# All score products over 128 rows, and the residual held in two tiles

## The chip, the core and the metric

The kernel runs on one core of a Trainium2 chip. The metric is the device time of one execution in microseconds (us).

## The reference

One decoder layer runs for a prompt of 1024 tokens and for 8 sequences of 4 new tokens each (1056 columns together). Differential attention and an RG-LRU recurrence share one input projection and one output projection; a gated ConvFFN follows. The prompt's attention, cut to what matters here:

```python
def diff_attn_block(q, k, v, mask, lam):
    s = jnp.einsum('bqhcd,bkhcd->bhcqk', q.astype(F32), k.astype(F32)) * (QK_SUB_DIM ** -0.5)
    s = jnp.where(mask, s, jnp.finfo(F32).min)
    p = jax.nn.softmax(s, axis=-1)
    p_diff = p[:, :, 0] - lam * p[:, :, 1]
    return jnp.einsum('bhqk,bkhd->bqhd', p_diff, v.astype(F32))
...
    m = jnp.concatenate([attn_out, lru_out], axis=-1) @ p['w_out']
    x = x + gt1 * m
```

There are 4 heads, each with 2 sub-heads `c` of 64 features. `x` is the residual; `gt1` comes from the modulation vector.

## The kernel before

A float32 matrix product is made of three products (`mm3`, lines 154 to 157): each operand is split into a high and a low part of type fp32r, and high x high, high x low and low x high are summed in PSUM. The stages follow one another: `front` normalises x, projects, runs the recurrence beside the projections, projects the values (`v_block`) and runs the prompt's attention; `output` runs the output projection with the sample attention beside it, and then the feed-forward part, which takes half of the time.

**The attention** runs over 16 groups `g`, four for each head; `pr = g % 4` is a pair of 128-query blocks. Each group has four score tiles `score(g, x, c)` with x and c in 0, 1, and each score tile is built of `pr + 1` pieces of up to 256 keys. A piece has two products. The first (line 744) contracts over 128 rows: the tile `QA` holds the 64 high features of a query and, in the other 64 rows, its low part, and `KA` holds the key's high part twice. The second (line 745) is high query x low key, and contracts over the 64 rows `me` of the sub-head alone. A bf16 product (line 746) adds the causal mask. That makes 160 products of each of the first two kinds.

A score tile lies in one of two PSUM buffers (`s_ps`). VectorE reduces its maximum (line 750), ScalarE takes the exponential (line 752), and with that the buffer is free. `combine` subtracts the two sub-heads on VectorE; `pv_T` transposes the result in TensorE, ScalarE and VectorE split it; `pv` multiplies with the values `vh`, `vl` into one PSUM buffer `pv_ps`, which ScalarE copies to `oT` and sends to DRAM (lines 795 to 797). Between the score tiles TensorE also does the projections of queries and keys three groups ahead (`qk_mm`, `qk_norm`) and the transposes of the next group (`qk_T`). `qk_norm` ends on GpSimd with the rotary part, which uses a scratch tile `rp` (lines 662 to 676); for pr = 2 the same is done for the 32 sample rows (`qk_ss`).

**The residual** is one tile `x2` of 128 x 8 x 1056. It stands where the values and the attention's tiles lie before, so `output` can load it only when the attention has ended (`x2_load`, line 1153). `accumulate` (line 1084) adds a product of the output projection to it. The first such group of products, `wo_first`, runs in the PSUM buffers of the score tiles during the end of the attention; the sample attention (`sa_pn`, `sa_ps`) takes these PSUM buffers after it.

What sets the order: the program is written in order, and a scheduler with a timeline model of its own then moves instructions on every engine, the DMA queue included. On the chip each engine runs its instructions strictly in the order that results.

Of the kernel before, what the change touches and what calls it, by code (L numbers as in the profile page):

```python
# [144 lines left out]
class Build:  # L145
# [56 lines left out]
    def front(self):  # L202
# [159 lines left out]
        lamb = self.load(lp, "lru_lambda", [128, 4])  # L362
        wgh = ada.tile([128, 2, 4, 128], F32R, name="wgh")
        wgl = ada.tile([128, 2, 4, 128], F32R, name="wgl")
        lco = lp.tile([128, 4, 27], F32, name="lco")
# [116 lines left out]
        e = lp.tile([128, 4, 4], F32, name="sp_e")  # L482
# [62 lines left out]
        evac(3, b)  # L545
        W.split_to(7)
# [41 lines left out]
        vpp = pool("v", side="right")  # L588
# [41 lines left out]
        SP.dma_start(a["lru_conv_o"], lco)  # L630
# [47 lines left out]
        PS, ST, QA, KA, KL = {}, {}, {}, {}, {}  # L678
        qbank = [lambda: bank("qk_ps", "mm", 6)]
# [15 lines left out]
        def qk_T(g):  # L695
# [9 lines left out]
            for c in range(2):  # L705
                S.activation(qa[me[c], c], b[me[c], 0], AF.Copy, scale=0.125)
            for c in range(2):
                S.activation(ka[me[c], c], b[me[c], 1], AF.Copy)
                S.activation(ka[me[1 - c], c], b[me[c], 1], AF.Copy)
# [24 lines left out]
        def score(g, x, c):  # L734
# [3 lines left out]
            me = slice(64 * c, 64 * c + 64)  # L738
            q = QA[g][:, c, x * 128:(x + 1) * 128]
            for kp in range(pr + 1):  # L740
# [4 lines left out]
                PE.matmul(o, q[me], KL[4 * h + kp][me, :w], start=False, stop=not last, skip_group_check=True)  # L745
# [5 lines left out]
            e = EX[g, x, c] = p.tile([128, 1024], F32, name="p_e", tag=f"p_e{c}", bufs=4 if c == 0 else 2)  # L751
# [29 lines left out]
        def pv(g, b):  # L781
# [12 lines left out]
            if last:  # L794
                ot = p.tile([128, 256], F32, name="oT", tag="oT", bufs=1)
# [21 lines left out]
        for g in range(NG):  # L817
# [82 lines left out]
        vpp.__exit__(None, None, None)  # L900
        self.psb = psp
# [170 lines left out]
    def output(self):  # L1072
        a, V, S, G, PE, SP, W = self.a, self.V, self.S, self.G, self.PE, self.SP, self.W
        pool, act_at = self.pool, self.act_at
        xpp = pool("x2", side="right")
        x2 = xpp.__enter__().tile([128, NK, T], F32, name="x2")
# [3 lines left out]
        def accumulate(b, m, i, gt, pl):  # L1080
# [3 lines left out]
            V.scalar_tensor_tensor(x2[:, m, t0:t0 + w], b[:, :w], gt[:, m, 0:1], x2[:, m, t0:t0 + w], op0=ALU.mult, op1=ALU.add)  # L1084
            if tw > w:
# [3 lines left out]
                V.tensor_tensor(x2[:, m, SEQ:], t, x2[:, m, SEQ:], op=ALU.add)  # L1089

        def norm2(i, env, acc):
# [15 lines left out]
            if tw > w:  # L1107
                ts = p.tile([128, NK, SAMP], F32, name="u2s", tag=tags[0], bufs=2)
                V.tensor_tensor(ts, x2[:, :, SEQ:], bc[:, None, w:tw].to_broadcast([128, NK, SAMP]), op=ALU.mult)
# [463 lines left out]
```

## Time and profile before

| | us |
|---|---|
| median of 3 runs | 1433.25 (1430.48 to 1434.02) |
| the profiled execution | 1431.46 |
| its span, first to last instruction | 1429.6 |
| TensorE busy | 1380.3 (97%) |
| VectorE, ScalarE, GpSimd busy | 810.8, 553.5, 427.3 |

The profile's engines are PE (TensorE matmul), PEld (its weight loads), DVE (VectorE), ACT (ScalarE), POOL (GpSimd) and SP (the queue that issues most DMAs). The recorded end of a matmul is modelled and overlaps the next one, so what a matmul costs is read from the distance of two starts, not from its duration. Stages in the span: up to 245 us projections and recurrence, 245 to 498 us the score tiles, then the end of the attention and the output projection up to 690 us, then the feed-forward part.

### The profile page before, as it was taken

The numbers are of one execution on the slowest core, as the hardware profiler recorded it, in microseconds if no ns is written. First come the engines' busy times: TensorE is split into PE (matmuls) and PEld (weight loads), VectorE is DVE, ScalarE is ACT, GpSimd is POOL, SyncE is SP. The second block draws the span as 40 slices with busy tenths as digits, with TensorE's granted clock in tenths as the row PEclk, the third lists the DMA queues.
The fourth block names the chain that finished last, engine by engine and source line by source line (L and its number), as shares of the span: only waits on it lengthen the run. The fifth ranks groups of instructions, "written<-read, shape, count | busy, mean of one in ns | idle before, by whom it ended". The sixth has DMA issues, their size and how long they took to land.

```text
span 1429.6 us, 23840 instructions
## 1 busy us (share of the span) xinstructions
PE 1380.3 (97%) x9520; PEld 1302.9 (91%) x9520; DVE 810.8 (57%) x1700; ACT 553.5 (39%) x981; POOL 427.3 (30%) x504
## 2 busy tenths in 40 slices
PE   3998999999999989999999999999999999999998
PEld 3898999788878777789999999999999999999998
DVE  5759534876667436578764545353545353635356
ACT  4366623554545532326723232314141414142411
POOL 1162114433334022413633232314141414142320
PEclk8999999998999899999999999999999999999999
DMA  8625351101011287502111010102020202020203
GB/s 337 253 91 182 144 186 56 50 16 45 20 42 58 70 299 245 187 29 72 45 45 60 30 60 31 60 30 60 30 70 20 75 16 75 15 74 17 73 16 133
DMA packets 51936, 121.99 MB, mean 85 GB/s; under 512 B 8274, under 2 KB 25554, under 8 KB 48754
## 3 DMA queue, kind: packets, MB, share of 16 engines
q1 hardware_dynamic: 46914, 115.73, 24.1%
q10 hardware_dynamic: 4912, 4.74, 1.0%
q8 instruction: 75, 1.23, 0.4%
q14 instruction: 35, 0.29, 0.1%
HBM read 106.51 MB, written 13.94 MB: 84 GB/s over the span
## 4 chain that ended last, share of the span: by engine, by line
PE 89%; DVE 6%; ACT 2%; DMA 2%; issue 1%; POOL 0%; SPq 0%; DVEq 0%; ACTq 0%; POOLq 0%
PE up L155 12%; PE up L156 12%; PE up L157 12%; PE dn L157 6%; PE dn L156 6%; PE dn L155 6%; PE s_ps L745 3%; PE qk_ps L155 3%; PE qk_ps L156 3%; PE qk_ps L157 3%; PE s_ps L744 2%; PE wo_ps L155 2%; PE wo_ps L157 2%; PE wo_ps L156 1%; PE qk_pt L774 1%
## 5 line engine op out<-in xcount | busy, mean ns | idle before, releaser
L60 POOL TENSOR_TENSOR w_lo<-w_raw,w_hi 128x1024 fp32r<-128x1024 f32 x90 | 223.7, 2494 | 592.4 <-ACT w_hi L59 500.9
L155 PE MATMUL up<-act_h,w_hi 128*128 128x384 f32 (+1 forms) x1056 | 341.4, 324 | 1.9 <-ACT act_h L1129 1.9
L157 PE MATMUL up<-act_h,w_lo 128*128 128x384 f32 (+1 forms) x1056 | 340.2, 323 | 0.8 <-DVE w_lo L60 0.8
L156 PE MATMUL up<-act_l,w_hi 128*128 128x384 f32 (+1 forms) x1056 | 340.8, 323 | 0.0
L1084 DVE SCALAR_TENSOR_TENSOR x<-dn,modT,x 128x384 f32<-128x384 f32 (+1 forms) x264 | 149.6, 570 | 167.9 <-PE dn L157 167.7
L1306 DVE SCALAR_TENSOR_TENSOR fy<-fx,conv_ffn_w,fy 128x1072 f32<-128x1072 f32 (+2 forms) x92 | 137.9, 1500 | 173.2 <-ACT fy L1304 171.9
L155 PEld LDWEIGHTS up<-act_h,w_hi 128*128 128x128 f32 x1056 | 197.9, 188 | 2.4 <-ACT act_h L1129 2.2
L157 PEld LDWEIGHTS up<-act_h,w_lo 128*128 128x128 f32 x1056 | 198.3, 188 | 1.1 <-DVE w_lo L60 1.1
L59 ACT ACTIVATE w_hi<-w_raw 128x1024 fp32r<-128x1024 f32 x94 | 98.0, 1057 | 261.7 <-PE dn L156 151.3
L156 PEld LDWEIGHTS up<-act_l,w_hi 128*128 128x128 f32 x1056 | 198.3, 188 | 0.0
L157 PE MATMUL dn<-hh,w_lo 128*128 128x384 f32 (+1 forms) x528 | 170.5, 323 | 0.0
L156 PE MATMUL dn<-hl,w_hi 128*128 128x384 f32 (+1 forms) x528 | 170.5, 323 | 0.0
L155 PE MATMUL dn<-hh,w_hi 128*128 128x384 f32 (+1 forms) x528 | 169.7, 321 | 0.0
L155 PEld LDWEIGHTS dn<-hh,w_hi 128*128 128x128 f32 x528 | 99.2, 188 | 0.0
L157 PEld LDWEIGHTS dn<-hh,w_lo 128*128 128x128 f32 x528 | 99.1, 188 | 0.0
L156 PEld LDWEIGHTS dn<-hl,w_hi 128*128 128x128 f32 x528 | 99.1, 188 | 0.0
L155 PE MATMUL qk_ps<-w_hi,act_h 128*128 128x256 f32 (+1 forms) x288 | 85.9, 298 | 0.0
L157 PE MATMUL qk_ps<-w_hi,act_l 128*128 128x256 f32 (+1 forms) x288 | 84.1, 292 | 0.0
L156 PE MATMUL qk_ps<-w_lo,act_h 128*128 128x256 f32 (+1 forms) x288 | 84.1, 292 | 0.0
L750 DVE TENSOR_REDUCE ls<-s_ps 128x1 f32<-128x128 f32 (+7 forms) x64 | 48.1, 755 | 54.1 <-PE s_ps L746 53.8
L155 PE MATMUL wo_ps<-act_h,w_hi 128*128 128x384 f32 (+1 forms) x192 | 62.7, 338 | 2.8 <-ACT p_e L752 1.1
L156 PE MATMUL wo_ps<-act_l,w_hi 128*128 128x384 f32 (+1 forms) x192 | 62.4, 326 | 0.0
(323 smaller groups left out, 2653.4 us busy)
## 6 DMA issues: line engine op xcount, KB each, us to landing
w_ada<-w_ada SPq DMA_DIRECT2D x24, 1024.0 KB, 6.3
w_raw<-w_up SPq DMA_DIRECT2D x44, 512.0 KB, 3.6
w_raw<-w_down SPq DMA_DIRECT2D x22, 512.0 KB, 3.5
w_raw<-w_in SPq DMA_DIRECT2D x20, 512.0 KB, 3.7
page<-cache_v SPq DMA_DIRECT2D x32, 256.0 KB, 5.0
xT<-xT SPq DMA_DIRECT2D x8, 528.0 KB, 7.9
w_raw<-w_out SPq DMA_DIRECT2D x8, 512.0 KB, 3.8
kp<-cache_k SPq DMA_DIRECT2D x16, 256.0 KB, 4.7
```

The costliest lines, as they stand in the source:

```text
L59: self.nc.scalar.activation(hi, self.raw[i], AF.Copy)
L60: (eng or self.nc.gpsimd).tensor_tensor(lo, self.raw[i], hi.bitcast(F32), op=ALU.subtract)
L155: self.PE.matmul(out, lh, rh, start=first, stop=False)
L156: self.PE.matmul(out, lh, rl, start=False, stop=False)
L157: self.PE.matmul(out, ll, rh, start=False, stop=last)
L744: PE.matmul(o, q, KA[4 * h + kp][:, c, :w], start=True, stop=False, skip_group_check=True)
L745: PE.matmul(o, q[me], KL[4 * h + kp][me, :w], start=False, stop=not last, skip_group_check=True)
L750: V.tensor_reduce(l[:, c:c + 1], b[:, :n], axis=AX.X, op=ALU.max, negate=True)
L774: PE.transpose(t[:, o:o + 128], PD[g, x][:, (2 * b + kk) * 128:(2 * b + kk + 1) * 128], ident)
L1084: V.scalar_tensor_tensor(x2[:, m, t0:t0 + w], b[:, :w], gt[:, m, 0:1], x2[:, m, t0:t0 + w], op0=ALU.mult, op1=ALU.add)
L1306: post.append(lambda c0=c0, c1=c1, j=j: V.scalar_tensor_tensor(y[:, c0:c1], x[:, c0 + j:c1 + j], fw[:, ci, j:j + 1], y[:, c0:c1], op0=ALU. ...
```

## The change

The low-key product gets a query tile `QZ` in which the 64 rows of the other sub-head are zero, so that it too contracts over 128 rows; two such tiles exist, zeroed once, and GpSimd copies the high query part into them in each group. The residual becomes two tiles of 128 x 4 x 1056. The first, `x2a`, takes the place of the values of heads 0 and 1, which are dead by group 9, and is loaded whole there; the second, `x2b`, is loaded in `output` in two pieces. To make room, the exponentials get tiles of their true width (still four and two of them), `oT` shares the one scratch tile of the rotary part (tag `rp`), and a few small tiles of the recurrence move to another pool, with their loads and arithmetic earlier. The line numbers of the changed kernel are larger by 4 to 18.

```diff
-        vh = [vp.tile([128, 8, 256], F32R, name=f"vh{b}") for b in range(2)]
-        vl = [vp.tile([128, 8, 256], F32R, name=f"vl{b}") for b in range(2)]
+        v01 = x2p.tile([128, 4 * T], F32R, name="v0", tag="v", bufs=1)[:, :4096]
+        v01 = [v01.rearrange("p (z t c) -> p z t c", z=2, t=8), vp.tile([128, 2, 8, 256], F32R, name="v1")]
+        vh, vl = ([t[:, z] for t in v01] for z in range(2))
...
+        QZ = [p.tile([128, 2, 256], F32R, name=f"QZ{i}") for i in range(2)]
+        for t in QZ:
+            G.memset(t.bitcast(F32), 0.0)
...
             for c in range(2):
+                G.tensor_copy(QZ[g % 2][me[c], c], qa[me[c], c])
...
-                PE.matmul(o, q[me], KL[4 * h + kp][me, :w], start=False, stop=not last, skip_group_check=True)
+                PE.matmul(o, qz, KL[4 * h + kp][:, :w], start=False, stop=not last, skip_group_check=True)
...
-            e = EX[g, x, c] = p.tile([128, 1024], F32, name="p_e", tag=f"p_e{c}", bufs=4 if c == 0 else 2)
+            e = EX[g, x, c] = p.tile([128, ((6, 8)[pr % 2 or c] - 1 + x) * 128], F32, name="p_e",
+                                     tag=f"p_e{c}{x}{'' if c else pr % 2}", bufs=1)
...
-                ot = p.tile([128, 256], F32, name="oT", tag="oT", bufs=1)
+                ot = p.tile([128, 256], F32, name="oT", tag="rp", bufs=1)
...
+            if g == 9:
+                self.x2 = [x2p.tile([128, 4, T], F32, name="x2a", tag="v", bufs=1)]
+                SP.dma_start(self.x2[0], a["xT"][0:4].rearrange("m p t -> p m t"))
...
-        x2_load(0, 4, 0, 384)
+        x2_load(0, 384)
...
-            x2_load(4, 4, 0, 384)
-            x2_load(0, 4, 384, T - 384)
-            x2_load(4, 4, 384, T - 384)
+            x2_load(384, T - 384)
```

Three places in the order of the built programs. On TensorE, at the end of the attention, before the change (`wo_ps` are the output projection's first group, `sa_pn` and `sa_ps` the sample attention):

```order
L155 MATMUL wo_ps<-act_h_66,w_hi 128x384
L156 MATMUL wo_ps<-act_l_67,w_hi 128x384
L157 MATMUL wo_ps<-act_h_66,w_lo 128x384
L992 MATMUL sa_pn<-ksT,qblk 32x32 x4
L998 MATMUL sa_ps<-kp,qblk 32x128
L992 MATMUL sa_pn<-ksT,qblk 32x32 x12
```

The same place with the change; the last two rows stand 31 rows behind the others, with products of the projection's second group between:

```order
L157 MATMUL wo_ps<-act_h_66,w_lo 128x384
L1201 MATMUL o_ms<-ident,le 12x128
L155 MATMUL wo_ps<-act_h_66,w_hi 128x384
L156 MATMUL wo_ps<-act_l_67,w_hi 128x384
...
L155 MATMUL wo_ps<-act_h_66,w_hi 128x384
L1007 MATMUL sa_pn<-ksT,qblk 32x32 x16
```

The sample attention's first products have moved behind products of the next projection group, which use other PSUM buffers.

On ScalarE, at the turn from group 6 to group 7, before the change (`oT` is the output of group 5, `qk_st` the projection for group 9):

```order
L752 ACTIVATE p_e_4004,ls_3946<-s_ps_3995,ls_3946 128x768
L796 ACTIVATE oT_4048<-pv_ps_3988 128x256
L797 DMA scr_o<-oT_4048 128x256
L649 ACTIVATE qk_st_4063<-qk_ps_3916 128x512
L651 ACTIVATE qk_sq_4065<-qk_ps_3916 128x512
L752 ACTIVATE p_e_4142,ls_4140<-s_ps_4130,ls_4140 128x896
```

And with the change:

```order
L762 ACTIVATE p_e_4025,ls_3965<-s_ps_4016,ls_3965 128x768
L653 ACTIVATE qk_st_4084<-qk_ps_3935 128x512
L655 ACTIVATE qk_sq_4086<-qk_ps_3935 128x512
L762 ACTIVATE p_e_4163,ls_4161<-s_ps_4151,ls_4161 128x896
L806 ACTIVATE oT_4069<-pv_ps_4009 128x256
L807 DMA scr_o<-oT_4069 128x256
```

The copy to `oT` now stands behind three more instructions, and in front of the exponential of group 7's second score tile.

On GpSimd, around the sample rows' rotary part in group 6 with the change (`QZ_2238` is the zero-padded query tile of group 7; before the change the three COPY rows are not there, and the rest stands in the same order):

```order
L716 COPY QZ_2237<-QA 64x256 x2
L60 TENSOR_TENSOR w_lo<-w_raw,w_hi 128x1024 x2
L716 COPY QZ_2238<-QA 64x256
L666 TENSOR_TENSOR qk_st<-qk_st,qk_ms 128x512
L716 COPY QZ_2238<-QA 64x256
L670 TENSOR_TENSOR qk_st<-qk_st,g_qk 128x256 x2
L666 TENSOR_TENSOR qk_ss<-qk_ss,qk_ms 32x256
```

The second copy for group 7 stands behind a normalisation that waits for VectorE.

## Rows read from the trace of the kernel before

**Rows 1.** The page: span, busy time by engine, and the chain that ended last.

```profile
span 1429.6 us, 23840 instructions
PE 1380.3 (97%) x9520; PEld 1302.9 (91%) x9520; DVE 810.8 (57%) x1700; ACT 553.5 (39%) x981; POOL 427.3 (30%) x504
PE 89%; DVE 6%; ACT 2%; DMA 2%; issue 1%; POOL 0%; SPq 0%; DVEq 0%; ACTq 0%; POOLq 0%
```

**Rows 2.** Windows: the score tiles, head 0's alone, the boundary; columns in the first line.

```profile
core 0: us, PE busy (x) PEld busy (x) DVE busy (x) ACT busy (x) POOL busy (x), PEclk, DMA share, GB/s
245.00:497.90 252.90, 250.39 (x1536) 208.16 (x1537) 176.56 (x512) 137.56 (x322) 85.22 (x130) 0.93 0.13 40
245.00:300.00 55.00, 54.06 (x345) 43.83 (x346) 44.07 (x125) 30.56 (x76) 21.11 (x31) 1.00 0.11 32
497.90:520.60 22.70, 17.58 (x117) 16.74 (x117) 8.70 (x15) 8.73 (x16) 6.29 (x10) 0.99 0.76 251
```

**Rows 3.** Timeline of TensorE, 441 to 446 us: start, duration, instruction.

```profile
441.03 0.28 PE L157 MATMUL qk_ps<-w_hi,act_l 128*128 128x256 f32 x1
...
442.45 0.28 PE L157 MATMUL qk_ps<-w_hi,act_l 128*128 128x256 f32 x1
...
443.96 0.28 PE L157 MATMUL qk_ps<-w_hi,act_l 128*128 128x256 f32 x1
444.08 0.28 PE L744 MATMUL s_ps<-KA,QA 128*128 128x256 f32 x1
444.29 0.38 PE L745 MATMUL s_ps<-KL,QA 64*128 64x256 f32 x1
444.60 0.49 PE L744 MATMUL s_ps<-KA,QA 128*128 128x128 f32 x2
445.02 0.38 PE L745 MATMUL s_ps<-KL,QA 64*128 64x256 f32 x1
445.33 0.33 PE L744 MATMUL s_ps<-KA,QA 128*128 128x128 f32 x1
```

**Rows 4.** Lines 744 and 745: count, duration (min, median, max), forms.

```profile
L744 PE MATMUL s_ps<-KA,QA x160: 219/364/581, 245.0 to 497.0; 128*128 128x256 f32 x128, 128*128 128x128 f32 x32
L745 PE MATMUL s_ps<-KL,QA x160: 322/381/579, 245.2 to 497.3; 64*128 64x256 f32 x128, 64*128 64x128 f32 x32
```

**Rows 5.** Windows of single groups: group 2 (head 0), group 7, group 15.

```profile
264.80:280.30 15.50, 15.17 (x96) 12.11 (x94) 15.23 (x41) 7.89 (x20) 9.05 (x9) 1.00 0.29 85
345.60:366.10 20.50, 20.50 (x105) 16.43 (x104) 12.65 (x33) 8.46 (x17) 7.30 (x15) 0.83 0.05 14
478.00:497.90 19.90, 19.90 (x84) 14.89 (x83) 7.67 (x13) 9.11 (x14) 0.00 (x0) 0.74 0.22 71
```

**Rows 6.** Waits in 245 to 500 us: total us, times, longest.

```profile
DVE ls L750 <- PE s_ps L746: 53.8, 40, 4.5
POOL qk_st L662 <- DVE qk_ms L142: 26.9, 6, 12.4
```

**Rows 7.** GpSimd groups, 245 to 500 us: busy us, mean ns, idle before.

```profile
L662 POOL TENSOR_TENSOR qk_st<-qk_st,qk_ms 128x512 f32<-128x512 f32 x14 | 14.6, 1045 | 90.2 <-DVE qk_ms L142 26.9 <-issue 21.3 <-ACT ksT L863 15.1
L675 POOL TENSOR_TENSOR rp<-qk_st,rope 128x64 f32<-128x64 f32 x14 | 4.5, 319 | 0.0
```

**Rows 8.** Timelines of ScalarE and GpSimd at 344 to 352 and 411 to 418 us.

```profile
344.27 0.38 ACT L796 ACTIVATE oT<-pv_ps 128x256 f32<-128x256 f32 x1 [3.56 <-PE pv_ps L157]
351.02 0.31 POOL L676 TENSOR_TENSOR qk_ss<-rp 32x64 f32<-32x64 f32 x1
411.65 0.38 ACT L796 ACTIVATE oT<-pv_ps 128x256 f32<-128x256 f32 x1 [3.57 <-PE pv_ps L157]
417.75 0.31 POOL L676 TENSOR_TENSOR qk_ss<-rp 32x64 f32<-32x64 f32 x1
```

**Rows 9.** Timeline of the boundary, 514 to 521 us.

```profile
514.26 0.39 SPq L1154 DMA_DIRECT2D x<-xT  x1
514.69 0.51 SPq L1150 DMA_DIRECT2D gsubT<-g_sub_col  x1
519.36 2.19 DVE L1084 SCALAR_TENSOR_TENSOR x<-wo_ps,modT,x 128x384 f32<-128x384 f32 x4 [7.10 <-DMA gsubT<-g_sub_col]
520.65 0.34 PE L992 MATMUL sa_pn<-ksT,qblk 128*32 128x32 f32 x8 [4.12 <-DVE x L1084]
```

More of the change, by code (lines that the diff above doesn't have):

```diff
@@ L361, in front @@
         lcs = self.load(lp, "state_lru_conv", [128, 4, NS, 3])
-        lamb = self.load(lp, "lru_lambda", [128, 4])
+        lamb = self.load(ada, "lru_lambda", [128, 4])
         wgh = ada.tile([128, 2, 4, 128], F32R, name="wgh")
         wgl = ada.tile([128, 2, 4, 128], F32R, name="wgl")
-        lco = lp.tile([128, 4, 27], F32, name="lco")
+        lco = ada.tile([128, 4, 27], F32, name="lco")
         lho = lp.tile([128, 4, 9], F32, name="lho")
@@ L481, in front @@
         sp = lp.tile([128, 2, 4], F32, name="sp")
-        e = lp.tile([128, 4, 4], F32, name="sp_e")
+        e = ada.tile([128, 4, 4], F32, name="sp_e")
         hb = lp.tile([128, 2, 4], F32, name="hb")
@@ L545, in front @@
         evac(3, b)
+        SP.dma_start(a["lru_conv_o"], lco)
         W.split_to(7)
@@ L587, in front @@
         self.pages = []
-        vpp = pool("v", side="right")
+        self.x2p = pool("v", side="right")
+        x2p = self.x2p.__enter__()
+        vpp = pool("stage", side="right")
         vp = vpp.__enter__()
-        vh = [vp.tile([128, 8, 256], F32R, name=f"vh{b}") for b in range(2)]
-        vl = [vp.tile([128, 8, 256], F32R, name=f"vl{b}") for b in range(2)]
+        v01 = x2p.tile([128, 4 * T], F32R, name="v0", tag="v", bufs=1)[:, :4096]
+        v01 = [v01.rearrange("p (z t c) -> p z t c", z=2, t=8), vp.tile([128, 2, 8, 256], F32R, name="v1")]
+        vh, vl = ([t[:, z] for t in v01] for z in range(2))
         def stage(name):
@@ L629, in front @@
         lpp.__exit__(None, None, None)
-        SP.dma_start(a["lru_conv_o"], lco)
         SP.dma_start(a["lru_h_o"], lho)
@@ L706, in qk_T @@
                 S.activation(qa[me[c], c], b[me[c], 0], AF.Copy, scale=0.125)
+            for c in range(2):
+                G.tensor_copy(QZ[g % 2][me[c], c], qa[me[c], c])
             for c in range(2):
@@ L737, in score @@
             b = sbank("s_ps")
-            me = slice(64 * c, 64 * c + 64)
-            q = QA[g][:, c, x * 128:(x + 1) * 128]
+            q, qz = (t[:, c, x * 128:(x + 1) * 128] for t in (QA[g], QZ[g % 2]))
             for kp in range(pr + 1):
@@ L900, in front @@
         vpp.__exit__(None, None, None)
+        self.x2bp = pool("x2b", side="right")
+        self.x2.append(self.x2bp.__enter__().tile([128, 4, T], F32, name="x2b"))
         self.psb = psp
@@ L1074, in output, with x2 @@
         pool, act_at = self.pool, self.act_at
-        xpp = pool("x2", side="right")
-        x2 = xpp.__enter__().tile([128, NK, T], F32, name="x2")
+        def x2(m, c0, c1):
+            return self.x2[m > 3][:, m - 4 * (m > 3), c0:c1]
         steps = Steps()
@@ L1108, in norm2 @@
                 ts = p.tile([128, NK, SAMP], F32, name="u2s", tag=tags[0], bufs=2)
-                V.tensor_tensor(ts, x2[:, :, SEQ:], bc[:, None, w:tw].to_broadcast([128, NK, SAMP]), op=ALU.mult)
+                for z, (m0, m1) in enumerate(((0, 4), (4, NK))):
+                    V.tensor_tensor(ts[:, m0:m1], self.x2[z][:, :, SEQ:],
+                                    bc[:, None, w:tw].to_broadcast([128, m1 - m0, SAMP]), op=ALU.mult)
             ut = None
@@ L1151, in output, with x2_load @@
         V.tensor_scalar(gsubT, gsubT, 1.0 - LAM0, None, op0=ALU.mult)
-        def x2_load(m, n, t0, tw):
-            SP.dma_start(x2[:, m:m + n, t0:t0 + tw], a["xT"][m:m + n, :, t0:t0 + tw].rearrange("m p t -> p m t"))
-        x2_load(0, 4, 0, 384)
+        def x2_load(t0, tw):
+            SP.dma_start(self.x2[1][:, :, t0:t0 + tw], a["xT"][4:, :, t0:t0 + tw].rearrange("m p t -> p m t"))
+        x2_load(0, 384)
         for m in range(4):
@@ L1238, in output @@
             self.lru_cat_stage(1, stage)
-            V.tensor_copy(x2[:1, 4:, 0:1], gsubT[:1, None].to_broadcast([1, 4, 1]))
-            V.tensor_copy(x2[:1, :, 384:385], gsubT[:1, None].to_broadcast([1, NK, 1]))
-            x2_load(4, 4, 0, 384)
-            x2_load(0, 4, 384, T - 384)
-            x2_load(4, 4, 384, T - 384)
+            for t0 in (384,):
+                V.tensor_copy(self.x2[1][:1, :, t0:t0 + 1], gsubT[:1, None].to_broadcast([1, 4, 1]))
+            x2_load(384, T - 384)
             for i in range(3):
@@ L1439, in output @@
             SP.dma_start(a["ffn_conv_o"], fo)
-        xpp.__exit__(None, None, None)
+        self.x2bp.__exit__(None, None, None)
+        self.x2p.__exit__(None, None, None)
         self.sqp.__exit__(None, None, None)
```

12 lines of the change are left out of this document (6 added, 6 removed).

## The prediction

> **What bounds the kernel now.** I read the page first: TensorE is busy 97% of the span, and the chain that ended last runs through it for 89% [rows 1]. So the question in each stage is what TensorE's own instructions cost, and where it stands still. Next the windows by stage: from 245 to 497.9 us, the score tiles, TensorE is busy 250.4 of 252.9 us, while VectorE has 176.6, ScalarE 137.6 and GpSimd 85.2 [rows 2]. TensorE is the bound there, but "busy" hides how well it is used; for that I took the timeline, start against start. From 441.03 to 442.45 us thirteen products of 256 columns over 128 rows follow each other: 12 steps in 1.42 us, 0.118 us each [rows 3]. A score product of the same width does not go at that pace: the first one starts at 444.08 as usual, the 64-row one follows after 0.21, and what follows that comes after 0.31; further on the 64-row product again takes 0.31 (445.02 to 445.33) [rows 3]. So what is slow is the passage from 128 rows to 64 and back, paid by both neighbours. The recorded durations say the same: no 64-row product is under 322 ns, and the 128-row one on the same tiles goes down to 219 [rows 4]. There are 160 of each [rows 4]. The last view is the boundary of attention and output projection: TensorE idles 4.12 us before the sample attention's first product, for a VectorE accumulation that itself waited 7.10 us for a small DMA behind the residual's load [rows 9].
>
> **The score products.** A pair met alone in other 128-row work takes 0.21 + 0.31 = 0.52 us and would take 0.24, so 0.28 is saved; inside a run of pairs both starts are 0.31 apart, 0.62 against 0.24, so 0.38. Times 160 that is 45 and 61 us. Runs and single pairs are mixed, and 32 pairs have only 128 columns; I take the middle, 0.33 a pair, **-53 us**. The new product has as many columns as before and adds no instruction on TensorE. One statement of the Trainium skill speaks against this term: "TensorE: Matmul & The Clock Gate" says in the section "Part 2: What happens when you issue a matmul" that the number of rows does not matter for a weight load, and in the table of "Why this matters for your kernels" that a product over 32 rows alone takes as long as one over 128; by that the term would be zero. The Trainium skill's "TensorEngine Tiling (Array Packing)", section "Key Properties", says on the other side that a change of the tiling mode drains the engine. The 0.31 against 0.118 above is on the side of the second, and no row here shows a 64-row product between 64-row ones, which would part the two.
>
> **What the other engines take of it.** With 53 us less, TensorE would need 200 us for this stage, and VectorE's 176.6 us are then 88% of it. Today VectorE waits 53.8 us in all for the last product of a score tile [rows 6]; that slack is what goes. The bounds: no loss, because in group 2 VectorE is busy 15.23 of 15.50 us and TensorE still 15.17 [rows 5]; and at the other end the share that VectorE reaches in head 0, its best whole head, 44.07 of 55 us or 80% [rows 2]: 176.6 / 0.80 = 221 us, a loss of 21. I take **+8**, nearer to the first, because VectorE's queue was laid out by a model and group 2 shows that it can run full.
>
> **The copies into QZ.** 32 copies of 64 x 256 on GpSimd. No such row exists; a two-operand instruction on 128 x 64 takes 319 ns and one on 128 x 512 takes 1045 [rows 7], so 10 to 33 us on an engine with 85 of 253 us busy. They hide beside TensorE's work for the group before. What is late if they don't: the copy for the second sub-head in pr = 3 stands behind a normalisation that waits for VectorE (26.9 us of such waits in all [rows 6]), and the score tiles of c = 1 and all behind them on TensorE wait for it. Zero to three places at up to 1.05 us each: **+1**.
>
> **oT on the rotary scratch tile.** The copy out of `pv_ps` now waits on ScalarE until GpSimd has finished with `rp`, and the exponentials, the next group's QA and KA stand behind it; TensorE waits for those when both score buffers are full. In group 6 the copy ran at 344.27 and the sample rows' rotary part ended at 351.33, 7.1 us later; in group 10, 411.65 and 418.06, 6.4 us [rows 8]. In the other heads the two meet or don't collide. The built order already puts the copy behind `qk_st`, `qk_sq` and an exponential, some 2 us. From 0 to 13.5 us; I take **+4**.
>
> **The clock.** The granted clock is 0.93 of 2.4 GHz over the stage [rows 2], and 0.83 and 0.74 in groups 7 and 15 [rows 5], the ones with most 64-row products; with levels of 1.2 and 2.4 GHz, 0.07 x 2 x 252.9 = 35 us ran at the lower one. At most half of that, 17 us, is lost, and the score products' part of it is in the term above already, so 0 to 10 us are left. If it fell for their pace, the change gives it back. Since it may fall again where TensorE waits for VectorE, I take **-3**.
>
> **The boundary.** The accumulations of `wo_first` go into `x2a`, which has been in place since group 9, so they no longer wait for the 0.79 MB of the first piece; and the sample attention's first products stand behind products of the next projection group, which use other PSUM buffers. The 4.12 us go: **-4** (0 to -5). `gsubT` still arrives late, but only VectorE's next instructions wait for it. The 2.2 MB load of `x2a` runs while DMA is 13% busy [rows 2], in the SP queue behind stores that wait for GpSimd today as well; nothing but the accumulations at the boundary needs it. The smaller p_e tiles rotate as before, and the recurrence's few early instructions replace the same ones later: both zero. The feed-forward part is built in the same order: zero.
>
> **The sum.** -53 + 8 + 1 + 4 - 3 - 4 = -47 us. The profiled execution took 1431.46 us (span 1429.6), which gives 1384.5; the median of the runs is 1.8 us above the profiled one, so 1386. A difference under 0.3%, 4 us, is about what a measurement of this kernel can't tell from none.
>
> **The rivals.**
>
> *VectorE and ScalarE become the bound.* The two in-order queues hand each other the two score buffers, and TensorE waits for the exponential of the tile before the last. For it: VectorE at 88%, and 13 us of ScalarE waits at the upper bound. Against it: group 2. At the upper ends, 21 + 3 + 13.5 in place of 8 + 1 + 4, the gain is 47 - 24.5 = 22 and the time 1411; 1402 to 1416 is its field.
>
> *The whole price comes back, and the clock with it.* No loss to other engines, 61 us for the products, 8 for the clock, 5 at the boundary: -74 us, 1359. Against it is VectorE: its 176.6 us leave no more than 76 for the stage. Field 1358 to 1370.
>
> *The row count isn't what costs.* If what TensorE pays lies in the score tile itself (its PSUM buffer, its accumulation), the products stay at 0.31, and the boundary alone is gained: 1429. For it: both neighbours of a 64-row product are in the same buffer as it. Against it: the projection's three products also accumulate in one buffer, at 0.118 [rows 3], and the 128-row score product started 0.12 after the product ahead. By the Trainium skill's "TensorE: Matmul & The Clock Gate" ("Why this matters for your kernels") this would be the outcome: no gain on 160 pairs.
>
> *Slower than before.* The shared `rp` tile, on ScalarE: if each `oT` waits for a rotary part as in groups 6 and 10, ScalarE stands 6.4 to 7.1 us, 6.75 in the mean, with the exponentials behind it. Up to 7 such stops take back the 47 us; with all 16, 108 us, less the 4 in the sum, the time is 1386 + 104 = 1490. Against it: in the groups with pr = 1 the rotary part ahead of the copy belongs to an earlier group, and the scheduler moved copies back; it decides from 8 full stops on.
>
> **How the numbers follow.** My forecast, 1370 to 1402, gets 0.66; the VectorE and ScalarE rival 0.18; the full price 0.08; the row count 0.04; slower 0.04. The range of 8 in 10 takes the forecast, most of the second and some of the third: 1368 to 1414. Faster by over 0.3% are the first three, 0.92; the row count lies at 4 us, half to each side but by its mechanism within 0.3%: 0.04; slower 0.04.
>
> **What would show it.** In the changed profile: starts of score products 0.12 us apart; the score stage at about 210 us with VectorE over 80% busy; granted clock above 0.93; ScalarE idle before `oT` put down to GpSimd under 10 us in all; no idle time before `sa_pn`. The prediction is wrong if the products stay 0.31 apart, if TensorE waits over 25 us in this stage for exponentials or for QZ, or if the output projection, whose order changed, loses more than the boundary gives.

## The result and the profile after

The changed kernel takes 1400.0 us (median of four runs, 1397.67 to 1400.61), the kernel before 1431.9 on the same chip: 0.9775 of it, 95% interval 0.9754 to 0.9796. That is 32 us gained where the sum said 47; 1400 lies in the range, at the slow end of the forecast's own field. The profiled execution has a span of 1398.2 us, 31.4 less than before [rows 1].

The page of the changed kernel, the rows that answer to [rows 1]: span, busy time by engine, and the chain that ended last.

```profile
span 1398.2 us, 23889 instructions
PE 1324.9 (95%) x9520; PEld 1279.5 (92%) x9520; DVE 831.2 (59%) x1700; ACT 552.3 (39%) x981; POOL 449.4 (32%) x538
PE 77%; DVE 13%; ACT 4%; DMA 3%; issue 2%; POOL 0%; SPq 0%; ACTq 0%; DVEq 0%; POOLq 0%
```

VectorE's share of the chain went from 6 to 13%, and VectorE and GpSimd are busy for 20 and 22 us more than before, though VectorE has as many instructions as before (1700) and GpSimd only 34 more (the 32 copies and two memsets). The windows of the changed kernel, with the columns of [rows 2], say where: the score tiles, the boundary, and the output projection up to the first product into `up`, with which the feed-forward part begins.

```profile
245.00:470.50 225.50, 197.85 (x1540) 188.11 (x1541) 191.55 (x510) 136.21 (x321) 102.63 (x161) 0.95 0.19 58
470.50:497.00 26.50, 23.76 (x150) 22.46 (x148) 13.55 (x25) 9.26 (x20) 4.86 (x10) 1.00 0.62 201
497.00:622.50 125.50, 124.61 (x1055) 102.81 (x1055) 80.34 (x250) 39.52 (x89) 40.72 (x36) 1.00 0.45 155
```

The first row against [rows 2]: the score stage is 27.4 us shorter (225.5 for 252.9). TensorE is busy for 52.5 us less (197.9 for 250.4), but stands still for 27.6 us where it stood for 2.5, so 25.1 us of the gain are lost again. VectorE's busy time didn't stay at 176.6; it is 191.6. Boundary and output projection together take 152.0 us; before, the first product into `up` started at 654.0, 156.1 us behind the end of the score stage. So 4.1 us came from there, and the feed-forward part is as long as before (775.7 and 775.6 us). The balance is -52.5 + 25.1 - 4.1 = -31.5 us.

The products themselves do what was forecast. TensorE's timeline in the last score tile, where such products had steps of 0.21 and 0.31 before [rows 3]:

```profile
469.38 0.28 PE L753 MATMUL s_ps<-KA,QA 128*128 128x256 f32 x1
469.50 0.28 PE L754 MATMUL s_ps<-KL,QZ 128*128 128x256 f32 x1
469.62 0.28 PE L753 MATMUL s_ps<-KA,QA 128*128 128x256 f32 x1
469.74 0.28 PE L754 MATMUL s_ps<-KL,QZ 128*128 128x256 f32 x1
469.86 0.28 PE L753 MATMUL s_ps<-KA,QA 128*128 128x256 f32 x1
```

Every start is 0.12 us behind the one ahead. Who ends TensorE's idle time in the stage stands in the view of waits of the changed kernel (total us, times, longest):

```profile
PE s_ps L753 <- DVE QA L721: 10.9, 5, 2.6
PE s_ps L753 <- ACT p_e L762: 4.5, 6, 1.8
PE qk_pt L784 <- DVE KL L724: 3.8, 3, 1.7
PE qk_ps L155 <- ACT gl L819: 3.1, 1, 3.1
PE pv_ps L155 <- ACT pTh L787: 2.2, 3, 1.7
```

Before, the longest entry was

```profile
PE s_ps L744 <- DVE QA L711: 1.6, 1, 1.6
```

and VectorE's wait for the end of a score tile, 53.8 us in [rows 6], is almost gone in the changed kernel:

```profile
DVE ls L759 <- PE s_ps L755: 7.9, 8, 2.7
```

Some 17 of TensorE's 27.6 us end with VectorE, most of the rest with ScalarE. What fills VectorE is the question of the experiments.

### The profile page after: what moved, and what is told of

It reads as the page before. It is cut to its first block, busy times and chain, and to the rows that moved or that the text cites. A ratio compares the mean times of both kernels' runs of the same rounds, so it can differ in the third digit from the quotient of the medians.

```text
span 1398.2 us, 23889 instructions
## 1 busy us (share of the span) xinstructions
PE 1324.9 (95%) x9520; PEld 1279.5 (92%) x9520; DVE 831.2 (59%) x1700; ACT 552.3 (39%) x981; POOL 449.4 (32%) x538
## 3 DMA queue, kind: packets, MB, share of 16 engines
q1 hardware_dynamic: 46386, 115.73, 24.5%
## 4 chain that ended last, share of the span: by engine, by line
PE 77%; DVE 13%; ACT 4%; DMA 3%; issue 2%; POOL 0%; SPq 0%; ACTq 0%; DVEq 0%; POOLq 0%
PE up L155 12%; PE up L156 12%; PE up L157 12%; PE dn L157 6%; PE dn L156 6%; PE dn L155 6%; PE wo_ps L155 1%; PE qk_ps L155 1%; PE qk_ps L156 1%; PE qk_ps L157 1%; PE wo_ps L156 1%; PE wo_ps L157 1%; DVE ls L759 1%; PE ada_ps L266 1%; PE v_ps L155 1%
## 5 line engine op out<-in xcount | busy, mean ns | idle before, releaser
L155 PEld LDWEIGHTS up<-act_h,w_hi 128*128 128x128 f32 x1056 | 197.9, 188 | 2.5 <-ACT act_h L1147 2.3
L1100 DVE SCALAR_TENSOR_TENSOR x2a<-dn,modT,x2a 128x384 f32<-128x384 f32 (+1 forms) x132 | 74.3, 567 | 98.5 <-PE dn L157 98.5
L1100 DVE SCALAR_TENSOR_TENSOR x2b<-dn,modT,x2b 128x384 f32<-128x384 f32 (+1 forms) x132 | 75.4, 573 | 69.4 <-PE dn L157 69.2
L155 PE MATMUL qk_ps<-w_hi,act_h 128*128 128x256 f32 (+1 forms) x288 | 85.8, 298 | 0.2 <-ACT qk_sq L655 0.2
L762 ACT ACTIVATE p_e<-s_ps,ls 128x128 f32<-128x128 f32 (+7 forms) x64 | 47.5, 743 | 47.1 <-DVE ls L759 42.3
```

Source lines behind the costliest of these rows:

```text
L155: self.PE.matmul(out, lh, rh, start=first, stop=False)
L762: S.activation(e[:, :n], b[:, :n], AF.Exp, bias=l[:, c:c + 1], accum_out=l[:, 2 + c:3 + c])
L1100: V.scalar_tensor_tensor(x2(m, t0, t0 + w), b[:, :w], gt[:, m, 0:1], x2(m, t0, t0 + w), op0=ALU.mult, op1=ALU.add)
```

## The experiments

Each edit is made in the program, and the scheduler then builds the order of the instructions anew, so an experiment can change the order on several engines besides what its edit says. One figure in the expectations needs a word: the *stretch* of VectorE. For every VectorE instruction of the score stage I took its duration, less that of the shortest tenth among those with the same tiles, operation and shape, and added up what was over 0.05 us; each excess is put down to the GpSimd line that ran beside it longest. It is 16.5 us before (8.9 beside the weight splits `w_lo`) and 35.2 in the changed kernel (16.5 beside `w_lo`, 16.2 beside the norms' multiplications and the rotary part, 2.5 beside the QZ copies).

**1. The residual's part alone.** QZ and its copies are left out of the changed kernel, and its products are those of before; the smaller `p_e` tiles and the shared `oT` tile stay. The product's line:

```diff
-                PE.matmul(o, qz, KL[4 * h + kp][:, :w], start=False, stop=not last, skip_group_check=True)
+                PE.matmul(o, q[me], KL[4 * h + kp][me, :w], start=False, stop=not last, skip_group_check=True)
```

> The changed kernel with the score products over 64 rows as before: no QZ and no copies into it, the rest of the change (residual in two tiles, oT on the rotary scratch tile, smaller p_e tiles) stays. If the two parts add up, this one gives only what the boundary and the output projection gave, 156.3 us before and 152.2 after from the last score product to the first up product: 4.1 us, so 1428, and a score stage of 252 to 253 us with TensorE at 250. Rival: the 2.2 MB load of x2a or the other order costs something in the score stage that the faster products hid or made up for: 1432 or more.

Measured 1439.6 us, 1.0058 (1.0038 to 1.0079) of before: 0.6% slower, clear of the noise. The window of its score stage:

```profile
246.20:507.70 261.50, 253.84 (x1529) 207.82 (x1529) 185.73 (x511) 138.24 (x324) 90.57 (x131) 0.92 0.20 63
```

The parts don't simply add up. Boundary and output projection give 2 us (154.1 from the last score product to the first `up`), but the score stage is 8.6 us longer: TensorE is idle for 7.7 us, where it was 2.5, and busy for 3.4 more at a lower clock (0.92). VectorE is busy for 9 us more, and its stretch is 26.0 us. Half of the loss, 4.6 us, was there when the ninth group began (at 371.9), ahead of the load of `x2a`, issued at 396.2.

**2. The products' part alone.** The kernel before with QZ, its copies, the 128-row products, the `p_e` tiles and `oT` as in the change:

```diff
-                PE.matmul(o, q[me], KL[4 * h + kp][me, :w], start=False, stop=not last, skip_group_check=True)
+                PE.matmul(o, qz, KL[4 * h + kp][:, :w], start=False, stop=not last, skip_group_check=True)
```

> The kernel before with the 128-row score products, the QZ copies, the smaller p_e tiles and oT on the rotary scratch tile, and the residual as before. If the parts add up: 1432 less the 27.4 us by which the score stage got shorter, 1404.5, with the 4.1 us of idle time before sa_pn still there. Rival: the x2a load or the order that comes with it is what holds the changed kernel's score stage at 225 us; then the stage is shorter here, 215 us, and the time 1394.

Measured 1403.9 us, 0.9804 (0.9778 to 0.9830). The sum held, though not by its parts: the stage is 220.8 us from the first to the last score product, where the changed kernel's is 225.2 counted alike, and the 4.5 us of idle time before `sa_pn` are back. The products' part is the whole gain but some 4 us, about as much as the two intervals leave open.

**3. 64-row products, grouped.** The kernel before, with the products of a score tile in another order. Every key piece marks the start of a sum here, so that the 64-row product of an even piece replaces the sum in place of adding to it: this kernel leaves out a part of the scores, which experiment 11 puts back.

```diff
-            for kp in range(pr + 1):
...
-                PE.matmul(o, q, KA[4 * h + kp][:, c, :w], start=True, stop=False, skip_group_check=True)
-                PE.matmul(o, q[me], KL[4 * h + kp][me, :w], start=False, stop=not last, skip_group_check=True)
+            for z in range(2):
+                for kp in range(pr + 1):
...
+                    if z == 0:
+                        PE.matmul(o, q, KA[4 * h + kp][:, c, :w], start=True, stop=False, skip_group_check=True)
+                    else:
+                        PE.matmul(o, q[me], KL[4 * h + kp][me, :w], start=False, stop=not last, skip_group_check=True)
```

> The kernel before with its 64-row products, but in each score tile all 128-row products first and then all 64-row ones: 64 passages from 128 rows to 64 and back in place of 160. If the passage costs, starts of 64-row products behind 64-row ones are 0.12 us apart, some 60% of the 52 us that TensorE saved in the changed kernel come without QZ (31 us of TensorE time), and the time is 1404 to 1414, as VectorE takes some of it. Rival: a product over 64 rows costs 0.31 us wherever it stands; then those starts are 0.31 apart. Second rival: rows don't matter, the score tile's own PSUM buffer is what costs; then all starts stay at 0.21 to 0.31 and the time at 1432.

Measured 1391.0 us, 0.9721 (0.9695 to 0.9746): faster than the changed kernel, without QZ. That is below the 1404 to 1414 expected. The stage is 213.0 us and TensorE is busy for 206.8 of them, 43.6 less than before, at a granted clock of 0.98 for 0.93. At half clock were 0.07 x 2 x 252.9 us before and 0.02 x 2 x 213.0 here; half of the difference, an estimated 13 us, is the clock's, and the other 30 are about the 31 expected of the passages. How the starts lie is shown under experiment 11.

**4. The square roots on GpSimd.** In the changed kernel:

```diff
-            V.tensor_scalar(ms, ms, 1.0 / 64, EPS, op0=ALU.mult, op1=ALU.add)
-            rsqrt_dve(V, y, t, ms)
+            G.tensor_scalar(ms, ms, 1.0 / 64, EPS, op0=ALU.mult, op1=ALU.add)
+            rsqrt_pool(G, y, t, ms)
```

> The changed kernel with the reciprocal square root of the query and key norms (11 small VectorE instructions a group) on GpSimd (14 instructions). If the score stage is held by VectorE, and by its small instructions that GpSimd's two-operand instructions stretch (35 us of such stretch in the changed kernel's stage, 16.5 before), VectorE's busy time falls from 192 to 140 to 150 us, TensorE's idle time in the stage from 27.6 to under 10, and the time to 1380 to 1386. Rival: the handing over of the two score buffers between VectorE and ScalarE is what costs, whatever VectorE does besides: TensorE's idle time stays over 20 and the time at 1395 to 1400. Second rival: GpSimd, then 160 us busy of 210, is late with the norms, and TensorE waits for QA as often as now: 1400 or more.

Measured 1380.6 us, 0.9643 (0.9618 to 0.9669). The stage is 205.2 us, VectorE busy for 150.3, TensorE idle for 12.9; the stretch is 10.3 us. This is what the expectation gave for a stage held by VectorE, but for the last 3 us of idle time. Of the 41 us that VectorE is rid of, 25 are stretch. GpSimd, busy for 157.7 us now, is hardly late: TensorE waits for it 0.9 us.

**5. The weight splits on VectorE.** In the changed kernel, for the nine units split in the score stage:

```diff
-                W.split_to((17, 19, 21, 23)[h])
+                W.split_to((17, 19, 21, 23)[h], V)
```

> The changed kernel with the low parts of the weights that are split in the score stage (w_lo, 9 instructions of 128x1024, 2.4 us each on GpSimd) made on VectorE. If GpSimd's long two-operand instructions hold VectorE's, the 16.5 us of stretch that lie beside w_lo go, and VectorE has 9 instructions of at most 1.6 us more (its combination of two 128x1024 tiles takes 1.61): 14.5 us. VectorE's busy time goes down by 2 us or more, the instructions of 2.2 to 2.4 us on 128x8 disappear, and the time is 1393 to 1400. Rival: the stretch is harmless, since VectorE had the time; then 14.5 us of new work on an engine at 85% make it slower, 1403 to 1414.

Measured 1397.4 us, 0.9756 (0.9734 to 0.9778). The stretch falls to 19.1 us, VectorE's busy time from 191.6 to 186.0, the stage from 225.5 to 218.0; part of that is given back behind it. The time lies in the field given for GpSimd holding VectorE, but its interval overlaps the changed kernel's, so the whole time decides nothing. GpSimd has 17 us less to do here (85.8) and VectorE 5.6, so the shorter stage alone doesn't tell which of the two counts; experiment 4, where GpSimd has 55 us more, does.

**6. The QZ copies on ScalarE.** In the changed kernel:

```diff
-                G.tensor_copy(QZ[g % 2][me[c], c], qa[me[c], c])
+                S.activation(QZ[g % 2][me[c], c], b[me[c], 0], AF.Copy, scale=0.125)
```

> The changed kernel with the QZ copies made by ScalarE straight from PSUM (as QA is, 0.38 us each, 30 in the stage) and not by GpSimd from QA. If GpSimd's copies only add to what holds VectorE, 2.5 us of stretch go, and ScalarE at 137 of 225 us takes 11.4 us more without harm: 1396 to 1400, TensorE's idle time in the stage still over 22 us. Rival: the copies delay GpSimd's norms and with them everything that VectorE and TensorE wait for; then idle time falls under 18 us and the time to 1390. Second rival: ScalarE is late with the exponentials: 1403 or more.

Measured 1405.8 us, 0.9823 (0.9798 to 0.9847), so GpSimd was not the wrong place for them. The time lies in the field of late exponentials, but in the profiled run TensorE waits 3.6 us for them, less than the 4.5 of the changed kernel. The runs go from 1400.6 us at a mean granted clock of 0.987 to 1418.2 at 0.972, and the profiled one is the slowest: (1 - 0.972) x 2 x 1416.3 = 79 us at half clock against 36, of which half, 21 us, would be lost if TensorE worked all that time, for 17.7 us between the runs. So the scatter goes with the clock and is of its size. That the clock causes it isn't shown: two runs of the changed kernel took 1400.0 us each, at 0.986 and at 0.981. No place of the 5.8 us could be made out.

**7. The residual's part when VectorE is relieved.** Experiment 2 with the edit of experiment 4.

> The 128-row products with the residual as before, and the reciprocal square roots on GpSimd: against the run of the changed kernel with them on GpSimd (1380.6) it tells what the residual's part of the change is worth when VectorE is relieved. If the 9 us that this part alone cost in the score stage came from VectorE's order and stretch, it gives here what the boundary gives, 4 to 7 us, and this kernel takes 1384 to 1388. Rival: the 2.2 MB load of x2a itself costs 4 to 9 us in the score stage (through the weights behind it in its queue, or the memory); then this kernel takes 1376 to 1381.

Measured 1382.9 us, 0.9667 (0.9649 to 0.9684), against 1380.6, 0.9643 (0.9618 to 0.9669), with the residual in two tiles. The intervals overlap: the residual's part is worth 2 to 3 us here, give or take 4. The loss of 7 us that it brought in experiment 1 doesn't show, which speaks for VectorE; whether it gives the 4 us of the boundary, or nothing, the noise leaves open.

**8. Grouped 64-row products with the residual in two tiles and the square roots on GpSimd.** Experiment 1 with the loops of experiment 11 and the edit of experiment 4.

> The changed kernel with 64-row products again, without QZ, but in each score tile first all 128-row products and then all 64-row ones, and the reciprocal square roots on GpSimd. If the passages from 128 rows to 64 and back cost and the rows don't, TensorE needs 8 us more than with 128 rows in the score stage (206.8 against 198.4 us busy so far), and GpSimd is rid of 12 us of copies: 1380 to 1388, about the changed kernel with those square roots on GpSimd (1380.6) or up to 8 us more. Rival: GpSimd, 158 us busy of 205 there, is what holds that kernel now; then the missing copies give more than the passages cost, 1372 to 1378.

Measured 1398.4 us, 0.9776 (0.9751 to 0.9801), longer than either expectation. TensorE is busy for 213.1 us, 6.5 more than in experiment 11, at a granted clock of 0.95 in the stage for 0.98: 0.05 x 2 x 222.8 = 22 us at half clock for 0.02 x 2 x 212.8 = 9, so an estimated 7 us lost. The runs (1395.4 to 1405.9) go with the mean clock (0.987 to 0.978) again. Why the clock fell in this order is open. Against experiment 4, the same kernel with 128-row products and 1380.6 us, TensorE is busy for 20.8 us more (213.1 for 192.3). Some 14 of them are the difference of 206.6, the grouped products of experiment 11, to 192.3 at the same clock (0.98), the rest those 7; it idles 3 us less. So with VectorE relieved, zeros are the better remedy by 18 us.

**9. Without the subtraction in the weight splits.** The changed kernel, with

```diff
-            (eng or self.nc.gpsimd).tensor_tensor(lo, self.raw[i], hi.bitcast(F32), op=ALU.subtract)
+            if low:
+                (eng or self.nc.gpsimd).tensor_tensor(lo, self.raw[i], hi.bitcast(F32), op=ALU.subtract)
+            else:
+                self.nc.gpsimd.memset(lo.bitcast(F32), 0.0)
```

> The changed kernel, leaving out part of the computation: the low parts of the 9 weight units that are split in the score stage are set to zero by GpSimd (one output, no operand) in place of the subtraction of two 128x1024 tiles, 2.4 us each. Nothing is added to VectorE. If those subtractions hold VectorE's two-operand instructions, 16.5 of its 35.2 us of stretch go, TensorE's idle time in the stage falls from 27.6 to 15 to 20 us, and the time to 1385 to 1392. Rival: VectorE's own work sets the pace and the stretch fills time that it has: idle time stays over 24 us, 1397 to 1401.

Measured 1379.2 us, 0.9642 (0.9618 to 0.9666): 21 us less than the changed kernel by the medians and 19 by the ratios, beyond what was expected. VectorE is busy for 171.0 us, its stretch is 16.2 (1.2 beside the memsets, 0.95 us each), and TensorE idle for 13.5; TensorE's busy time is 8 us lower too, at a clock of 0.97.

**10. Both reliefs.** Experiments 4 and 5 together.

> The changed kernel with both reliefs: the reciprocal square roots on GpSimd (1380.6 alone) and the low parts of the weights in the score stage on VectorE (1397.4 alone, against 1400.0). VectorE then has some 160 of 205 us, GpSimd some 137. If what is left of TensorE's idle time (13 us) comes from VectorE held by w_lo and from GpSimd's length, it falls under 9 us: 1374 to 1379. Rival: what is left is the chain of exponentials and buffers, whatever these two do: 1379 to 1383. Second rival: the subtractions at the head of VectorE's queue wait for weights and hold the score tiles: 1384 or more.

Measured 1380.1 us, 0.9640 (0.9621 to 0.9659): no more than experiment 4 alone. TensorE stays idle for 15.4 us, with VectorE at 157.5 and GpSimd at 146.8 us. The first rival: below the 171.0 us that VectorE has in experiment 9, less of its load no longer shortened the stage in these runs. The longest idle times that are left end with `p_e` (4.3 us) and `pTh` (2.8), the others are under 2 us each; what would remove them wasn't tried.

**11. Grouped alone, with the sums mended.** Experiment 3 with

```diff
-                        PE.matmul(o, q, KA[4 * h + kp][:, c, :w], start=True, stop=False, skip_group_check=True)
+                        PE.matmul(o, q, KA[4 * h + kp][:, c, :w], start=kp % 2 == 0, stop=False, skip_group_check=True)
```

> The kernel before with grouped 64-row products, and the start of accumulation marked on even key pieces alone; in the earlier grouped run each piece marked it, so that the 64-row product of an even piece overwrote the 128-row one's sum and was not added to it. If only the order of the products counts, the time is that of the earlier run, 1388 to 1394, with a score stage of 213 us. Rival: overwriting was what made the 64-row products cheap: 64-row starts go back to 0.3 us apart and the time over 1410.

Measured 1390.4 us, 0.9719 (0.9695 to 0.9743), the time of experiment 3. TensorE's timeline of this kernel; "x3" stands for three products in a row, with the time from the first one's start to the last one's end:

```profile
435.21 0.51 PE L746 MATMUL s_ps<-KA,QA 128*128 128x256 f32 x3
435.56 0.49 PE L777 MATMUL qk_pt<-ident,p_e 128*128 128x128 f32 x3
435.98 0.62 PE L748 MATMUL s_ps<-KL,QA 64*128 64x256 f32 x3
436.53 0.23 PE L749 MATMUL s_ps<-mkb,idb 128*128 128x128 bf16 x1
```

In the trace the three 64-row products start at 435.98, 436.20 and 436.32: the second is 0.22 us behind the first, the third 0.12 behind the second. It is so over the whole stage. Of 67 steps between two 64-row products of 256 columns, the 36 that stand first in their run have a median of 0.22, and the 31 behind them one of 0.118, the step of the 128-row ones; from 128 rows to 64 it is 0.209, and from 64 to the 128-row mask product 0.209. So a passage and its way back are paid at three starts here, 0.29 us in all, about what a pair met alone costs. Behind the first step the row count costs nothing, as the Trainium skill's "TensorE: Matmul & The Clock Gate" has it in the table that the prediction cites; the passage costs, on the side of the Trainium skill's "TensorEngine Tiling (Array Packing)", section "Key Properties". Each page is right on its own point.

**12. The load of x2a later.** Experiment 1 with

```diff
-            if g == 9:
+            if g == 14:
```

> The residual's part of the change alone (1439.6 us with 64-row products), with the 2.2 MB load of x2a issued in group 14 and not in group 9. If the load is what costs the 9 us in the score stage, the stage is back at 252 to 254 us and the time at 1428 to 1432, unless the accumulations at the boundary now wait for it. Rival: the other order of instructions, with VectorE stretched for 26 us (16.5 before) and TensorE's clock lower for 7.7 us more, is what costs: the stage stays over 257 us and the time at 1434 to 1442.

Measured 1440.5 us, 1.0073 (1.0046 to 1.0100), but the load is issued at 395.9 us, where it was issued at 396.2 in experiment 1: the order that the scheduler built put it back. So this repeats experiment 1 and says nothing on the load. VectorE, GpSimd and ScalarE have the same order in both runs. Whether the load costs a part of the 8.6 us stays open, apart from the 4.6 that were lost ahead of it.

## Why the prediction was right, and what it sized wrongly

The score stages side by side, from the first to the last score product (before and the changed kernel: the windows shown), in us; the times are medians:

| kernel | time | stage | TensorE busy | idle | VectorE | GpSimd |
|---|---|---|---|---|---|---|
| before | 1431.9 | 252.9 | 250.4 | 2.5 | 176.6 | 85.2 |
| changed | 1400.0 | 225.5 | 197.9 | 27.6 | 191.6 | 102.6 |
| 1: residual's part alone | 1439.6 | 261.5 | 253.8 | 7.7 | 185.7 | 90.6 |
| 2: products' part alone | 1403.9 | 220.8 | 196.3 | 24.5 | 186.7 | 103.2 |
| 5: `w_lo` on VectorE | 1397.4 | 218.0 | 196.5 | 21.5 | 186.0 | 85.8 |
| 9: no subtraction | 1379.2 | 203.4 | 189.9 | 13.5 | 171.0 | 91.3 |
| 4: square roots on GpSimd | 1380.6 | 205.2 | 192.3 | 12.9 | 150.3 | 157.7 |
| 10: both reliefs | 1380.1 | 204.3 | 188.9 | 15.4 | 157.5 | 146.8 |
| 11: grouped 64 rows | 1390.4 | 212.8 | 206.6 | 6.2 | 179.1 | 86.9 |
| 8: as 4, but grouped 64 rows | 1398.4 | 222.8 | 213.1 | 9.7 | 147.6 | 146.3 |

**The score products, -53, and the clock, -3.** Right in mechanism, and nearly in size: TensorE's busy time fell by 52.5 us for the 56 of both. The steps are 0.12 as forecast, and experiment 11 shows that it is the passage that had cost. The granted clock is 0.95 for 0.93, so 0.07 x 2 x 252.9 = 35 us at half clock became 0.05 x 2 x 225.5 = 23. Half of the difference is 6 us; it is in the 52.5 already.

**What the other engines take, +8, with QZ, +1, and oT, +4.** Here the sum failed in size: 13 us were forecast and 25.1 measured. Experiment 2, with the residual as before, has 24.5 us of idle time for 27.6, so some 3 us may be the residual's part; as no wait for QZ or `oT` shows among TensorE's, the other 22 fall on the +8, beyond its bound of 21. The step that failed is "VectorE's 176.6 us are then 88% of it": it took VectorE's busy time as given, and it became 191.6. The shorter stage alone is not the reason. In experiment 11 VectorE, GpSimd and ScalarE have the instructions of the stage in the same order as before, and with a stage 40 us shorter VectorE is busy for 2.5 us more:

```profile
242.30:455.10 212.80, 206.62 (x1534) 186.06 (x1534) 179.05 (x512) 136.49 (x322) 86.91 (x130) 0.98 0.15 45
```

GpSimd's added work is not the reason alone either: in experiment 6, without the QZ copies on GpSimd, it is busy for 91.4 us, and VectorE still for 190.2. And experiment 1 has VectorE at 185.7 in a longer stage. What the changed kernel and these two share, and experiment 11 doesn't have, are the smaller `p_e` tiles, the shared `oT` tile, and with them another order of the instructions on every engine. So the added busy time is put down to which VectorE instructions meet which of GpSimd's; that is argued from these runs, and no run changed the order of these two engines alone. The timelines of VectorE and GpSimd in group 6 of the changed kernel show how (start, duration, instruction); first VectorE, then GpSimd:

```profile
326.85 0.17 DVE L141 TENSOR_TENSOR qk_ms<-qk_ms 128x8 f32<-128x8 f32 x1
327.05 2.38 DVE L142 SCALAR_TENSOR_TENSOR qk_ms<-qk_ms 128x8 f32<-128x8 f32 x1
329.46 2.30 DVE L140 TENSOR_TENSOR qk_ms<-qk_ms 128x8 f32<-128x8 f32 x1
331.80 0.83 DVE L759 TENSOR_REDUCE ls<-s_ps 128x1 f32<-128x640 f32 x1
332.54 0.16 DVE L141 TENSOR_TENSOR qk_ms<-qk_ms 128x8 f32<-128x8 f32 x1
```

```profile
327.02 4.73 POOL L60 TENSOR_TENSOR w_lo<-w_raw,w_hi 128x1024 fp32r<-128x1024 f32 x2 [5.84 <-ACT w_hi L59]
```

Two instructions on eight columns, 0.16 us each at other times, take 2.38 and 2.30 us, and end when the two splits on GpSimd end. The maximum of the next score tile stands behind them, then its exponential, and TensorE, which had finished the projection products by 331.8, starts its next score tile at 333.59. The Trainium skill states the rule in "SBUF — State Buffer", section "SBUF: two separate sides": VectorE instructions with two SBUF inputs and GpSimd instructions that read SBUF shut each other out of a shared port pair, for the whole instruction. The trace agrees: the 2.4 us ones are held, and the memsets of experiment 9, which read nothing, account for 1.2 us of stretch where the subtractions had 16.5. The groups of VectorE's small instructions show the sum of it: count, busy us, mean ns. Before:

```profile
L142 DVE SCALAR_TENSOR_TENSOR qk_ms<-qk_ms 128x8 f32<-128x8 f32 x41 | 9.9, 242 | 0.6
L762 DVE SCALAR_TENSOR_TENSOR ls<-ls,lam__1624 128x1 f32<-128x1 f32 x31 | 9.0, 290 | 0.3
L141 DVE TENSOR_TENSOR qk_ms<-qk_ms 128x8 f32<-128x8 f32 x41 | 8.6, 211 | 0.5
L140 DVE TENSOR_TENSOR qk_ms<-qk_ms 128x8 f32<-128x8 f32 x41 | 6.5, 160 | 0.4
```

The changed kernel:

```profile
L142 DVE SCALAR_TENSOR_TENSOR qk_ms<-qk_ms 128x8 f32<-128x8 f32 x41 | 13.2, 321 | 0.5
L140 DVE TENSOR_TENSOR qk_ms<-qk_ms 128x8 f32<-128x8 f32 x41 | 11.9, 290 | 0.5
L772 DVE SCALAR_TENSOR_TENSOR ls<-ls,lam__1625 128x1 f32<-128x1 f32 x31 | 11.9, 384 | 0.4
L141 DVE TENSOR_TENSOR qk_ms<-qk_ms 128x8 f32<-128x8 f32 x41 | 9.9, 241 | 0.7
```

Experiment 9 (line numbers 3 higher):

```profile
L775 DVE SCALAR_TENSOR_TENSOR ls<-ls,lam__1625 128x1 f32<-128x1 f32 x30 | 10.1, 336 | 0.2
L143 DVE TENSOR_TENSOR qk_ms<-qk_ms 128x8 f32<-128x8 f32 x41 | 7.6, 186 | 0.6
L144 DVE TENSOR_TENSOR qk_ms<-qk_ms 128x8 f32<-128x8 f32 x41 | 7.1, 174 | 0.7
L145 DVE SCALAR_TENSOR_TENSOR qk_ms<-qk_ms 128x8 f32<-128x8 f32 x41 | 6.7, 163 | 0.7
```

The four together have 34.0 us before, 46.9 in the changed kernel, and 31.5 without the subtraction. Experiments 4 and 9 take load from VectorE in two ways, and each gets some 20 us back; in 4 GpSimd is 55 us busier, so it is VectorE's time that counts and not GpSimd's. In 9, with VectorE at 171.0 us, near the 176.6 that the forecast counted on, TensorE is idle for 11 us more than before, near the forecast's 13. Two limits: experiment 9 also shortens GpSimd by 11 us, and in 4, 5 and 9 the order was built anew (in 9 only 370 of VectorE's 507 instructions follow one another as in the changed kernel). So the 20 us are not shown to come from the stretch alone; a luckier order is a rival that no run parts from it.

The copies into QZ and `oT` cost TensorE nothing that the waits show. ScalarE's idle time ahead of `oT` never ended with GpSimd; the instructions of `oT` on the shared tile, in the changed kernel:

```profile
L806 ACT ACTIVATE oT<-pv_ps x16: 358/385/405, 265.2 to 488.4; 128x256 f32<-128x256 f32 x16
...
its engine sat idle before it (us, times) until:
  PE pv_ps L157: 3.8, 3
  issue: 2.2, 1
who waited for it (us, times):
...
  POOL rp L677: 5.3, 1
```

The wait went the other way: GpSimd's rotary part waited once, 5.3 us, for the store of `oT`.

**The boundary, -4.** Measured 4.1, and the wait before `sa_pn` is gone. But the part of the change that brings it is not free: alone it made the kernel slower by 7 to 9 us (experiments 1 and 12), in the score stage. The prediction put the order and the smaller tiles at zero ("the smaller p_e tiles rotate as before, and the recurrence's few early instructions replace the same ones later"), and `oT`, whose shared tile these two runs have too, at 4. In the changed kernel 4.4 us of its stage stand against the two tiles, their load and the order that comes with them (experiment 2 has the smaller `p_e` tiles and the shared `oT` as well). Which of these costs wasn't parted.

**The rivals.** VectorE as the bound, put at 1402 to 1416, described what happened better than the forecast did; only ScalarE's part in it, the waits ahead of `oT`, didn't come. Of the prediction's own tests the steps, the clock, `oT` and `sa_pn` came out as said; the stage is 225 us for the 210 forecast. TensorE's 27.6 us of idle time are more than the 25 named as a sign of being wrong, but only 4.5 of them end with exponentials. The products gave 3.5 us less than forecast and the other engines took 12 more, both to the same side. The time came out 2 us from the forecast's upper end, which is this rival's lower one; that it lies well inside the stated range is owed to the share of this rival in it.

## What to carry to other kernels

What a short product costs on TensorE is read from the starts of its neighbours: here it was the passage between 128 and 64 rows. Putting like beside like (1390 us) gained more than filling the rows with zeros (1400) as long as VectorE held the zero-filled kernel back; with its square roots on GpSimd, zeros won (1380.6 against 1398.4). Before an engine's idle time is counted as slack for others, look at which of its instructions run beside whose: VectorE's busy time is no constant when its order against GpSimd's changes. Moving its small instructions away was worth another 20 us here (1380.6).

## What was not expected of the hardware

- A passage to 64 rows is paid beyond the first start: 0.209 us into a run of them, 0.22 for the next one, 0.209 out, for 0.118 each. Where 64 and 128 rows alternate each start takes 0.31, so that a pair costs 0.38 us more there and 0.28 met alone.
- One 128x1024 subtraction on GpSimd can turn a 0.16 us VectorE instruction into one of 2.38.
- With the same products in another order, and VectorE, GpSimd and ScalarE in the same one, the granted clock in the score stage went from 0.93 (before) to 0.98 (experiment 11); between runs of one kernel the mean clock differed by up to 0.015, with 17.7 us between them (experiment 6).
